# Sliding-window attention with the values as the stationary operand: two heads side by side on 64 array columns each, and the division by the denominators moved to ScalarE

## The chip, the cores and the metric

The program runs on one NeuronCore of a Trainium2 chip, in one launch. The metric is the device time in microseconds (us) of one execution. TensorE (PE in the profile, its weight loads PEld), VectorE (DVE), ScalarE (ACT), GpSimd (POOL) and SyncE (SP) each run their own instructions strictly in the order of the program and wait for one another through semaphores.

## The reference, cut to what matters

Four layers on 256 tokens of width 1024: two of a first kind, then two "hybrid" layers, each with a gated delta-rule branch, a sliding-window branch and a feed-forward part. The change is in the sliding-window branch, which has 16 query heads of width 64 on 2 key/value heads, blocks of 128 tokens, a window of 128 and one sink logit per head:

```python
def swa_sink_branch(q_in, k_in, v_in, positions, sinks):
    ...
    scores = jnp.einsum('bnqhgd,bnkhd->bnhgqk', qb, kw) * (SW_HEAD_DIM ** -0.5)
    ...
    scores = jnp.where(mask, scores, -jnp.inf)
    sink = sinks.astype(jnp.float32).reshape(SW_KV_HEADS, G)[None, None, :, :, None, None]
    m = jnp.maximum(jnp.max(scores, axis=-1, keepdims=True), sink)
    p = jnp.exp(scores - m)
    probs = p / (jnp.sum(p, axis=-1, keepdims=True) + jnp.exp(sink - m))
    o = jnp.einsum('bnhgqk,bnkhd->bnqhgd', probs.astype(vw.dtype), vw)
    return o.reshape(B, S, SW_Q_W)

def hybrid_layer_2(x, positions, ...):
    ...
    y_b = swa_sink_branch(sw_q, sw_k, sw_v, positions, sw_sinks) @ w_up_sw
```

## The kernel before

Every large product takes a 128x128 stationary tile and streams up to 512 columns. A weight matrix comes from memory in pieces of 256 rows by 512 columns (`raw`). ACT rounds a piece to `hi` (L284) and DVE takes the rest `lo` (L285), and the activations are kept as such a pair too (`lhi`, `llo`). A product is then three matmuls, L312 to L314 in `mm3`, or L353 to L355 in `proj_w`. Four split pieces are kept (`NSPLIT`).

Python writes the order of all engines ahead of time. `at(k, fn)` puts `fn` on a list for `k` steps from now, `tick(0.5)` after each three or six matmuls moves the clock on and emits what is due, and `feed` splits the next weight piece when a buffer is free. So attention, the delta rule and the projections stand interleaved in one fixed order per engine. `wk` hands out three PSUM buffers in turn, to scores (`sc`), transposes (`tp`, `pt`) and the delta rule's products (`pg`, `inv`) alike: PE writes the next one only when the reader of the third last is done.

A hybrid layer (`layer2`) calls `swa(g)` for the two groups of 8 heads; I number a layer's heads 0 to 15. For each head, `windowed` schedules four functions: `s_` (scores on PE at L495 and L496, mask and maximum on DVE at L500, `nm` at L1276), 1.5 steps later `e_` (two exponentials on ACT at L1284, which also leave the row sums in `den`; the sink's exponential `es` at L1287; their sum on POOL), at 2.8 `t_` (three transposes on PE at L507, copied by ACT at L509 to `ptS`), and at 3.7 `v_`. The columns of `e` are the keys of three pairs of blocks: query block 1 with key blocks 0 and 1, and query block 0 with key block 0. `v_` calls `pv_mm`: three matmuls with a 128x128 block of probabilities stationary and the 64 value columns streaming. After every fourth head DVE takes the reciprocal of the eight denominators (L1303) and multiplies `o` into `y` (L1305, twice); `y` lies in the buffer named `tok`. After the eighth head `to_lh` turns `y` with four PE transposes per token block (L371) and splits it (ACT L376, DVE L378) into `sw["lb"]`, the operand of the product with `w_up_sw`.

At the same places run the delta rule's steps: on DVE `eights` and `corner` (L1138 to L1155), `spread` (L1158), and the convolution's taps (six instructions of L993, which continue what ACT starts at L990); on PE `level_z` (L1167). The queries' own copies into `qk` alternate between ACT (L461) and DVE (L462).

Of the kernel before, what the change touches and what calls it, by code (L numbers as in the profile page):

```python
# [12 lines left out]
F32 = mybir.dt.float32  # L13
# [64 lines left out]
def body(ctx: ExitStack, tc: tile.TileContext, I, out, upto=None):  # L78
# [52 lines left out]
    def wk(shape, name="wk", tag="wk", bufs=3):  # L131
        return ps.tile(shape, F32, name=name, tag=tag, bufs=bufs)
# [98 lines left out]
    def at(k, fn):  # L231
        heapq.heappush(due, (clk[0] + k, seq[0], fn))
        seq[0] += 1
# [16 lines left out]
    def tiny(n, name="tiny", bufs=4):  # L250
        return sm.tile([128, n], F32, name=name, tag=f"{name}{n}", bufs=bufs)
# [202 lines left out]
    def into_stack(dst, r, tabs):  # L454


        def then(p, cols, t):
            for i in range(2):
                a, b = halves(i)
                h = dst[a, i:8:2, cols]  # L460
                S.activation(h, p[a], AF.Copy)  # L461
                V.tensor_tensor(out=dst[b, i:8:2, cols], in0=p[a], in1=h.bitcast(F32), op=ALU.subtract)  # L462
        return turned(r, tabs, then, 4)
# [40 lines left out]
    def probs_T(p):  # L504
        pt = wk([128, 384], "pt")
        for j in range(3):
            T.transpose(pt[:, j * 128:(j + 1) * 128], p[:, j * 128:(j + 1) * 128], ident)  # L507
        r = sm.tile([128, 384], F32, name="ptS", tag="ptS", bufs=2)
        S.activation(r, pt, AF.Copy)  # L509
        return r  # L510

    def pv_mm(o1, o0, pt, v, cols):
        T.matmul(o1, pt[:, 0:128], v[:, 0, cols], start=True, stop=False)
        T.matmul(o1, pt[:, 128:256], v[:, 1, cols], start=False, stop=True)
        T.matmul(o0, pt[:, 256:384], v[:, 0, cols], start=True, stop=True)

    def e_tile():
        return sm.tile([128, 384], F32, name="e", tag="e", bufs=3)

    def by_block(ap, n=4):  # L520
        return ap.rearrange("p (h t) -> p h t", t=2)
# [353 lines left out]
    def layer2(l, last):  # L875
# [388 lines left out]

        lane = [0.0]

        def windowed(q, g, y):
            st = {}

            def s_(h):  # L1270
                if h % 4 == 0:
                    st["den", h // 4] = tiny(8, "den")
                s, mx = scores(q[:, h, :], kTs[0][:, g, :], kTs[1][:, g, :], tb_("bs"))
                nm = tiny(2, "nm")
                hs = 8 * g + h
                V.tensor_scalar(nm, mx, -0.125, nsink[:, hs:hs + 1], op0=ALU.mult, op1=ALU.min)  # L1276
                st["s", h] = s, nm

            def e_(h):
                den, i, hs = st["den", h // 4], h % 4, 8 * g + h  # L1280
                s, nm = st.pop(("s", h))
                e = e_tile()
                for j, (a, b) in enumerate(SPL):
                    S.activation(e[:, a:b], s[:, a:b], AF.Exp, bias=nm[:, j:j + 1], scale=0.125,  # L1284
                                 accum_out=den[:, 2 * i + j:2 * i + j + 1])
                es = tiny(2, "es")
                S.activation(es, nm, AF.Exp, bias=sinks[:, 16 * l + hs:16 * l + hs + 1])  # L1287
                G.tensor_tensor(out=den[:, 2 * i:2 * i + 2], in0=den[:, 2 * i:2 * i + 2], in1=es, op=ALU.add)
                st["p", h] = e

            def t_(h):
                st["pt", h] = probs_T(st.pop(("p", h)))

            def v_(h):
                hh, i = h // 4, h % 4
                if i == 0:
                    st["o"] = wk([128, 4, 2, 64], "o", "o", 1)
                o = st["o"]
                pv_mm(o[:, i, 0, :], o[:, i, 1, :], st.pop(("pt", h)), vS, slice(64 * g, 64 * g + 64))
                if i < 3:  # L1300
                    return
                rd = tiny(8, "rd")
                V.reciprocal(rd, st["den", hh])  # L1303
                for j in range(2):
                    V.tensor_tensor(out=y[:, 1 - j, 256 * hh:256 * hh + 256].rearrange("p (h d) -> p h d", d=64),  # L1305
                                    in0=o[:, :, j, :],
                                    in1=rd.rearrange("p (h t) -> p t h", t=2)[:, j, :, None].to_broadcast([128, 4, 64]),
                                    op=ALU.mult)
                if hh == 1:
                    for t in range(2):  # L1310
                        at(1.6 + t, lambda t=t: to_lh(sw["lb"], y[:, t, :], 4 * g, t))

            for h in range(8):
                k = max(4, lane[0] - clk[0])
                at(k, lambda h=h: s_(h))
                at(k + 1.5, lambda h=h: e_(h))
                at(k + 2.8, lambda h=h: t_(h))
                at(k + 3.7, lambda h=h: v_(h))
                lane[0] = clk[0] + k + 2.1

        m1, fins, end = [], [], 0.0
# [7 lines left out]
        def swa(g):  # L1329
            q = qk_tile([8, 256], F32R)  # L1330
            if g == 0:
                sw["lb"] = new_lh()
            y, evac = into_stack(q, None, rope2)
            proj(lh, evac)
            windowed(q, g, y)

        for hh in range(2):
            qkn = dn_qk(hh)
# [206 lines left out]
```

## Time and profile before

| what | value |
|---|---|
| time of three runs, median | 1740.27 us (1738.24 to 1742.22) |
| the profiled execution: its time, its span | 1741.27 us, 1739.5 us |
| PE busy, PEld busy | 1705.6 us (98%), 1484.6 us (85%) |
| DVE, ACT, POOL busy | 1169.9 us (67%), 996.4 us (57%), 268.1 us (15%) |
| mean granted clock of TensorE | 0.994 |

The span runs from the first to the last instruction that the profiler recorded, and the execution's own time is 1.8 us longer. "Busy" counts instructions in flight. PE's matmuls overlap one another, so what a matmul costs is read from the distance between starts, and not from its duration. A matmul on plain fp32 operands shows as two records, each with a weight load of its own; a transpose shows as one.

### The profile page before, as it was taken

What the parts mean: (1) busy time and instruction counts of PE and PEld (TensorE: products, weight loads), DVE (VectorE), ACT (ScalarE), POOL (GpSimd) and SP (SyncE); (2) the same over time, 40 slices, a digit from 0 to 9 for tenths busy, and PEclk for the clock granted to TensorE, in tenths of its full rate; (3) what the DMA queues carried; (4) which work ended last, traced back from release to release, by engine and by line L of the source; (5) the groups of instructions that cost most, each with busy time, mean ns of one, the idle gap of its engine ahead of it and who ended that gap; (6) DMA issues with size and microseconds to landing.
All of it is one profiled execution on the core that took longest, in us unless ns stands there. A gap on an engine that the chain in (4) does not pass through costs nothing.

```text
span 1739.5 us, 26865 instructions
## 1 busy us (share of the span) xinstructions
PE 1705.6 (98%) x9865; PEld 1484.6 (85%) x9865; DVE 1169.9 (67%) x2189; ACT 996.4 (57%) x1786; POOL 268.1 (15%) x507
## 2 busy tenths in 40 slices
PE   8999999999999999999999999999999999999998
PEld 6788888888888888898889889998998888889997
DVE  5676776666777766788585676555788584775554
ACT  6666665466666654665665455445565666464443
POOL 2112321031123200320220000000320210010000
PEclk9999999999999999999999999999999999999999
DMA  6655465466655565554332655665554333646564
GB/s 206 196 173 167 152 189 173 159 195 181 177 164 155 172 192 174 168 166 134 96 104 86 197 167 182 194 193 170 160 170 140 87 102 93 198 158 195 184 184 140
DMA packets 158932, 282.27 MB, mean 162 GB/s; under 512 B 20560, under 2 KB 28496, under 8 KB 158800
## 3 DMA queue, kind: packets, MB, share of 16 engines
q1 hardware_dynamic: 157840, 277.83, 53.0%
q0 software_dynamic: 720, 2.62, 0.4%
q8 instruction: 78, 1.28, 0.3%
q14 instruction: 54, 0.44, 0.1%
q10 hardware_dynamic: 240, 0.09, 0.0%
HBM read 270.53 MB, written 1.59 MB: 156 GB/s over the span
## 4 chain that ended last, share of the span: by engine, by line
PE 51%; DVE 5%; issue 1%; ACT 1%; POOL 0%; DMA 0%; DVEq 0%; POOLq 0%; SPq 0%; ACTq 0%
PE acc L314 6%; PE acc L312 6%; PE acc L313 6%; PE acc L353 5%; PE acc L354 5%; PE acc L355 5%; PE facc L313 3%; PE facc L312 3%; PE facc L314 3%; DVE lo L285 2%; DVE hcv L993 1%; PE inv L1177 1%; PE inv L1167 1%; PE tp L371 1%; PE pt L507 1%
## 5 line engine op out<-in xcount | busy, mean ns | idle before, releaser
L285 DVE TENSOR_TENSOR lo<-raw,hi 128x1024 fp32r<-128x1024 f32 (+1 forms) x504 | 617.3, 1231 | 343.9 <-ACT hi L284 328.1
L284 ACT ACTIVATE hi<-raw 128x1024 fp32r<-128x1024 f32 (+1 forms) x504 | 527.3, 1052 | 357.5 <-PE acc L314 149.0
L312 PE MATMUL acc<-hi,lhi 128*128 128x512 f32 (+1 forms) x1344 | 550.4, 410 | 1.2 <-ACT lhi L385 1.2
L314 PE MATMUL acc<-hi,llo 128*128 128x512 f32 (+1 forms) x1344 | 526.2, 392 | 0.4 <-DVE llo L388 0.3
L313 PE MATMUL acc<-lo,lhi 128*128 128x512 f32 (+1 forms) x1344 | 524.2, 390 | 0.6 <-DVE lo L285 0.5
L314 PEld LDWEIGHTS acc<-hi,llo 128*128 128x128 f32 x1344 | 253.5, 189 | 57.4 <-DVE llo L388 3.4
L313 PEld LDWEIGHTS acc<-lo,lhi 128*128 128x128 f32 x1344 | 255.3, 190 | 41.3 <-DVE lo L285 2.0
L312 PEld LDWEIGHTS acc<-hi,lhi 128*128 128x128 f32 x1344 | 255.0, 190 | 39.7 <-ACT lhi L385 1.4
L353 PE MATMUL acc<-lhi,hi 128*128 128x256 f32 x832 | 239.1, 287 | 0.0
L355 PE MATMUL acc<-lhi,lo 128*128 128x256 f32 x832 | 235.4, 283 | 0.0
L354 PE MATMUL acc<-llo,hi 128*128 128x256 f32 x832 | 235.4, 283 | 0.0
L353 PEld LDWEIGHTS acc<-lhi,hi 128*128 128x128 f32 x832 | 159.5, 192 | 1.2 <-issue 0.4
L354 PEld LDWEIGHTS acc<-llo,hi 128*128 128x128 f32 x832 | 159.5, 192 | 0.7
L355 PEld LDWEIGHTS acc<-lhi,lo 128*128 128x128 f32 x832 | 159.4, 192 | 0.0
L312 PE MATMUL facc<-hi,fh 128*128 128x512 f32 x256 | 99.8, 390 | 0.0
L313 PE MATMUL facc<-lo,fh 128*128 128x512 f32 x256 | 99.8, 390 | 0.0
L314 PE MATMUL facc<-hi,fl 128*128 128x512 f32 x256 | 99.6, 389 | 0.0
L509 ACT ACTIVATE ptS<-pt 128x384 f32<-128x384 f32 x80 | 39.2, 490 | 82.0 <-PE pt L507 81.8
L546 POOL TENSOR_SCALAR pf<-pss 128x1 f32<-128x1 f32 x8 | 3.7, 458 | 467.6 <-ACT pj L860 467.6
L500 DVE CUSTOM_DVE_ANT_0 s<-sc,tab 128x256 f32<-128x256 f32 x192 | 60.4, 352 | 11.2 <-PE sc L496 10.6
L993 DVE SCALAR_TENSOR_TENSOR hcv<-acc,cw,hcv 128x255 f32<-128x255 f32 (+1 forms) x144 | 58.2, 475 | 1.5 <-ACT hcv L990 1.4
L314 PEld LDWEIGHTS facc<-hi,fl 128*128 128x128 f32 x256 | 48.1, 188 | 10.1
(306 smaller groups left out, 2206.9 us busy)
## 6 DMA issues: line engine op xcount, KB each, us to landing
raw<-in_w_in_dram SPq DMA_DIRECT2D x272, 512.0 KB, 3.8
raw<-in_w_ff_dram SPq DMA_DIRECT2D x128, 512.0 KB, 4.4
raw<-in_w_proj_a_dram SPq DMA_DIRECT2D x16, 512.0 KB, 3.9
raw<-in_w_proj_b_dram SPq DMA_DIRECT2D x16, 512.0 KB, 3.7
raw<-in_w_out_dram SPq DMA_DIRECT2D x16, 512.0 KB, 3.7
raw<-in_w_up_sw_dram SPq DMA_DIRECT2D x16, 512.0 KB, 3.7
raw<-in_w_up_dn_dram SPq DMA_DIRECT2D x16, 512.0 KB, 3.7
raw<-in_w_o_dram SPq DMA_DIRECT2D x16, 512.0 KB, 3.8
```

What stands on the lines that cost most here:

```text
L284: S.activation(hi[:, :, :o], raw[:, :, :o], AF.Copy)
L285: V.tensor_tensor(out=lo[:, :, :o], in0=raw[:, :, :o], in1=hi[:, :, :o].bitcast(F32), op=ALU.subtract)
L312: T.matmul(a, lh[0][:, c, sl], hi[:, cc, :n], start=first, stop=False)
L313: T.matmul(a, lh[0][:, c, sl], lo[:, cc, :n], start=False, stop=False)
L314: T.matmul(a, lh[1][:, c, sl], hi[:, cc, :n], start=False, stop=last)
L353: T.matmul(a, hi[:, c % 2, sl], lh[0][:, c, :], start=(c == 0 and m % 2 == 0), stop=False)
L354: T.matmul(a, hi[:, c % 2, sl], lh[1][:, c, :], start=False, stop=False)
L355: T.matmul(a, lo[:, c % 2, sl], lh[0][:, c, :], start=False, stop=(c == 7 and m % 2 == 1))
L371: T.transpose(p[:, a, :], src[:, a * 128:(a + 1) * 128], ident)
L500: V.tensor_tensor_reduce(s[:, a:b], sc[:, a:b], bias[:, a:b], 1.0, FMIN, ALU.add, ALU.max, accum_out=mx[:, j:j + 1])
L509: S.activation(r, pt, AF.Copy)
L993: V.scalar_tensor_tensor(ha[:, m, d:], a[:, m, :256 - d], tap(3 - d, m), ha[:, m, d:], op0=ALU.mult, op1=ALU.add)
```

## The change

`v_` now works on pairs of heads. The values (128 keys x 64) are stationary, the turned probabilities stream: for key block 0 the two query blocks that use it in one matmul of 256 columns, for key block 1 one matmul of 128 columns. The first head of a pair writes PSUM partitions 0 to 63, that is columns 0 to 63 of the array, the second one partitions 64 to 127. The result stands with the head's width on partitions already, in the layout of `sw["lb"]`, so `y`, `to_lh` and its transposes go. ACT and DVE split `o` straight into `sw["lb"]` (L1327, L1328).

Since queries are now on the free axis, the division comes earlier, on the probabilities, where queries are still on partitions: a new step `r_` (DVE: add `es` and `den`, L1292, then the reciprocal, L1293) and a new step `n_` (ACT: `e` times that reciprocal in place, in two pieces, L1299). `t_` moves from 2.8 to 4.6 steps, `v_` from 3.7 to 5.6. `e` has four buffers. POOL's addition goes. No DMA is added, removed or moved.

```diff
-        return sm.tile([128, 384], F32, name="e", tag="e", bufs=3)
+        return sm.tile([128, 384], F32, name="e", tag="e", bufs=4)
...
-                G.tensor_tensor(out=den[:, 2 * i:2 * i + 2], in0=den[:, 2 * i:2 * i + 2], in1=es, op=ALU.add)
+                st["p", h] = e, es
+
+            def r_(h):
+                rd, i, (e, es) = tiny(2, "mx"), h % 4, st["p", h]
+                V.tensor_tensor(out=rd, in0=st["den", h // 4][:, 2 * i:2 * i + 2], in1=es, op=ALU.add)
+                V.reciprocal(rd, rd)
+                st["p", h] = e, rd
+
+            def n_(h):
+                e, rd = st["p", h]
+                for j, (a, b) in enumerate(SPL):
+                    S.activation(e[:, a:b], e[:, a:b], AF.Copy, scale=rd[:, j:j + 1])
                 st["p", h] = e
...
-                pv_mm(o[:, i, 0, :], o[:, i, 1, :], st.pop(("pt", h)), vS, slice(64 * g, 64 * g + 64))
-                if i < 3:
+                if h % 2 == 0:
                     return
-                rd = tiny(8, "rd")
-                V.reciprocal(rd, st["den", hh])
...
+                for blk in range(2):
+                    for i, pt in enumerate(pts):
+                        w = o[64 * i:64 * i + 64, pr, :]
+                        if blk == 0:
+                            T.matmul(w.rearrange("p (t c) -> p t c", t=2), vS[:, 0, 64 * g:64 * g + 64], pt[:, 0:3:2, :],
+                                     start=True, stop=False)
+                        else:
+                            T.matmul(w[:, 0:128], vS[:, 1, 64 * g:64 * g + 64], pt[:, 1, :], start=False, stop=True)
...
-                        at(1.6 + t, lambda t=t: to_lh(sw["lb"], y[:, t, :], 4 * g, t))
+                    S.activation(hi, p, AF.Copy)
+                    V.tensor_tensor(out=lo, in0=p, in1=hi.bitcast(F32), op=ALU.subtract)
...
-                at(k + 2.8, lambda h=h: t_(h))
-                at(k + 3.7, lambda h=h: v_(h))
+                at(k + 2.6, lambda h=h: r_(h))
+                at(k + 3.0, lambda h=h: n_(h))
+                at(k + 4.6, lambda h=h: t_(h))
+                at(k + 5.6, lambda h=h: v_(h))
```

Three places show where the new steps come to stand. All are in the first hybrid layer where its first group of heads ends and the second begins. On DVE, from the `nm` of head 9 on, before:

```order
L1276 TENSOR_SCALAR nm<-mx,nsink 128x2
L993 SCALAR_TENSOR_TENSOR hcv<-acc,cw_80,hcv 128x255 x2
L993 SCALAR_TENSOR_TENSOR hcv<-acc,cw_80,hcv 128x254 x2
L993 SCALAR_TENSOR_TENSOR hcv<-acc,cw_80,hcv 128x253 x2
L285 TENSOR_TENSOR lo<-raw,hi 128x1024
L378 TENSOR_TENSOR llo<-tp,lhi 128x4x128
L1158 TENSOR_TENSOR Xi<-Y,tab 128x512
```

and now:

```order
L1276 TENSOR_SCALAR nm<-mx,nsink 128x2
L993 SCALAR_TENSOR_TENSOR hcv<-acc,cw_80,hcv 128x255 x2
L993 SCALAR_TENSOR_TENSOR hcv<-acc,cw_80,hcv 128x254 x2
L993 SCALAR_TENSOR_TENSOR hcv<-acc,cw_80,hcv 128x253 x2
L1292 TENSOR_TENSOR mx<-den,es 128x2
L1293 RECIPROCAL mx<-mx 128x2
L285 TENSOR_TENSOR lo<-raw,hi 128x1024
L1158 TENSOR_TENSOR Xi<-Y,tab 128x512
L1328 TENSOR_TENSOR llo<-o,lhi 128x2x128 x2
```

The denominators of head 8 stand behind the taps and right ahead of the weights' `lo`; heads 7 and 9 have the same neighbour behind them. On ACT, the same place, from the exponentials of head 8 on, before:

```order
L1284 ACTIVATE e,den<-s,nm 128x256
L1284 ACTIVATE e,den<-s,nm 128x128
L1287 ACTIVATE es<-nm,bv_sw_sinks_336 128x2
L990 ACTIVATE hcv<-acc,cw_80 128x256 x2
L509 ACTIVATE ptS<-pt 128x384
L284 ACTIVATE hi<-raw 128x1024
L376 ACTIVATE lhi<-tp 128x4x128
```

and now:

```order
L1284 ACTIVATE e,den<-s,nm 128x256
L1284 ACTIVATE e,den<-s,nm 128x128
L1287 ACTIVATE es<-nm,bv_sw_sinks_336 128x2
L509 ACTIVATE ptS<-pt 128x384
L990 ACTIVATE hcv<-acc,cw_80 128x256 x2
L1299 ACTIVATE e<-e,mx 128x256
L1299 ACTIVATE e<-e,mx 128x128
L284 ACTIVATE hi<-raw 128x1024
L1327 ACTIVATE lhi<-o 128x2x128 x2
```

The division of head 8 stands right ahead of the `hi` of the same weight piece. On PE, where the projection changes from `proj_w` to `proj`, before:

```order
L355 MATMUL acc<-lhi,lo 128x256
L507 MATMUL pt<-ident,e 128x128 x3
L312 MATMUL acc<-hi,lhi 128x512
L313 MATMUL acc<-lo,lhi 128x512
L314 MATMUL acc<-hi,llo 128x512
L371 MATMUL tp<-ident,tok 128x128 x4
L312 MATMUL acc<-hi,lhi 128x512
L313 MATMUL acc<-lo,lhi 128x512
L314 MATMUL acc<-hi,llo 128x512
L513 MATMUL o<-vS,ptS 128x64
L514 MATMUL o<-vS,ptS 128x64
L515 MATMUL o<-vS,ptS 128x64
```

and now:

```order
L355 MATMUL acc<-lhi,lo 128x256
L312 MATMUL acc<-hi,lhi 128x512
L313 MATMUL acc<-lo,lhi 128x512
L314 MATMUL acc<-hi,llo 128x512
L1317 MATMUL o<-ptS,vS 64x256 x2
L1320 MATMUL o<-ptS,vS 64x128 x2
L312 MATMUL acc<-hi,lhi 128x512
L313 MATMUL acc<-lo,lhi 128x512
L314 MATMUL acc<-hi,llo 128x512
```

Head 8's three transposes have moved 9 product matmuls down, past the next scores, the four transposes of `y` are gone, and two heads' value products are four instructions in a row.

## Rows read from the trace of the kernel before

**Rows 1.** The profile's page: busy time, and the granted clock in 40 slices.
```profile
PE 1705.6 (98%) x9865; PEld 1484.6 (85%) x9865; DVE 1169.9 (67%) x2189; ACT 996.4 (57%) x1786; POOL 268.1 (15%) x507
...
PEclk9999999999999999999999999999999999999999
```
**Rows 2.** Timeline of PE near 945: start us, duration us, instruction.
```profile
945.01 0.39 PE L314 MATMUL acc<-hi,llo 128*128 128x512 f32 x1
945.25 0.33 PE L513 MATMUL o<-vS,ptS 128*128 128x64 f32 x2
...
945.83 0.47 PE L312 MATMUL acc<-hi,lhi 128*128 128x512 f32 x1
946.14 0.39 PE L313 MATMUL acc<-lo,lhi 128*128 128x512 f32 x1
946.37 0.40 PE L314 MATMUL acc<-hi,llo 128*128 128x512 f32 x1
```
**Rows 3.** Timeline of PE near 949: four transposes of `y`.
```profile
948.65 0.40 PE L314 MATMUL acc<-hi,llo 128*128 128x512 f32 x1
948.89 0.60 PE L371 MATMUL tp<-ident,tok 128*128 128x128 f32 x4
...
949.56 0.39 PE L313 MATMUL acc<-lo,lhi 128*128 128x512 f32 x1
```
**Rows 4.** Timeline of PE near 780: fp32 matmuls of 256 and 128 columns.
```profile
780.09 0.60 PE L1085 MATMUL pg<-qk 128*128 128x256 f32 x2
780.52 0.38 PE L1086 MATMUL pg<-qk 128*128 128x128 f32 x2
...
780.86 0.28 PE L354 MATMUL acc<-llo,hi 128*128 128x256 f32 x1
780.98 0.28 PE L355 MATMUL acc<-lhi,lo 128*128 128x256 f32 x1
```
**Rows 5.** Timeline near 1263: the same two shapes on 8 array columns.
```profile
1262.89 0.60 PE L942 MATMUL tp<-tab,gd 128*8 128x256 f32 x2
...
1263.33 0.38 PE L943 MATMUL tp<-tab,gd 128*8 128x128 f32 x2
...
1263.86 0.28 PE L354 MATMUL acc<-llo,hi 128*128 128x256 f32 x1
```
**Rows 6.** Busy us of the engines in two stretches of 10 us, from 890.
```profile
890.00:900.00 10.00, 9.89 (x75) 8.85 (x74) 9.04 (x22) 7.59 (x19) 1.31 (x2) 1.00 0.31 71
900.00:910.00 10.00, 9.14 (x63) 8.04 (x62) 9.96 (x25) 6.33 (x19) 1.29 (x2) 1.00 0.33 101
```
**Rows 7.** Timeline of PE at two waits; in brackets idle time and releaser.
```profile
886.83 0.63 PE L446 MATMUL tp<-ident,tok 128*128 128x128 f32 x4 [0.33 <-DVE mx L500]
...
903.65 0.52 PE L507 MATMUL pt<-ident,e 128*128 128x128 f32 x3 [0.86 <-DVE llo L378]
```
**Rows 8.** Timeline of DVE from 895 to 910.
```profile
895.62 0.42 DVE L500 CUSTOM_DVE_ANT_0 s<-sc,tab 128x256 f32<-128x256 f32 x1
...
897.57 0.20 DVE L1303 RECIPROCAL rd<-den 128x8 f32<-128x8 f32 x1
897.87 0.76 DVE L1305 TENSOR_TENSOR tok<-o,rd 128x256 f32<-128x256 f32 x2
...
902.82 0.69 DVE L378 TENSOR_TENSOR llo<-tp,lhi 128x512 fp32r<-128x512 f32 x1
...
909.50 0.42 DVE L500 CUSTOM_DVE_ANT_0 s<-sc,tab 128x256 f32<-128x256 f32 x1
```
**Rows 9.** Timeline of ACT: a scaling by columns, and three rows of 893 to 898.
```profile
769.21 0.80 ACT L1081 ACTIVATE D<-D,cj 128x256 f32<-128x256 f32 x2 [2.85 <-POOL cj L1036]
...
893.38 1.05 ACT L284 ACTIVATE hi<-raw 128x1024 fp32r<-128x1024 f32 x1
...
896.56 0.51 ACT L1284 ACTIVATE e<-s,nm 128x256 f32<-128x256 f32 x1 [2.13 <-DVE nm L1276]
...
897.64 0.82 ACT L990 ACTIVATE hcv<-acc,cw 128x256 f32<-128x256 f32 x2
```

More of the change, by code (lines that the diff above doesn't have):

```diff
@@ L1265, in layer2, with windowed @@
         lane = [0.0]
-        def windowed(q, g, y):
+        def windowed(q, g):
             st = {}
@@ L1289, in e_ @@
+            def n_(h):
+                e, rd = st["p", h]
+                for j, (a, b) in enumerate(SPL):
+                    S.activation(e[:, a:b], e[:, a:b], AF.Copy, scale=rd[:, j:j + 1])
                 st["p", h] = e
             def t_(h):
-                st["pt", h] = probs_T(st.pop(("p", h)))
+                st["pt", h] = probs_T(st.pop(("p", h))).rearrange("p (a c) -> p a c", a=3)
             def v_(h):
-                hh, i = h // 4, h % 4
-                if i == 0:
-                    st["o"] = wk([128, 4, 2, 64], "o", "o", 1)
@@ L1298, in v_ @@
-                o = st["o"]
-                pv_mm(o[:, i, 0, :], o[:, i, 1, :], st.pop(("pt", h)), vS, slice(64 * g, 64 * g + 64))
-                if i < 3:
-                    return
-                rd = tiny(8, "rd")
-                V.reciprocal(rd, st["den", hh])
[L1304 to L1308, printed above, removed]
@@ L1309, in v_ @@
-                if hh == 1:
-                    for t in range(2):
-                        at(1.6 + t, lambda t=t: to_lh(sw["lb"], y[:, t, :], 4 * g, t))
+                if h % 2 == 0:
+                    return
+                if h % 4 == 1:
+                    st["o"] = wk([128, 2, 256], "o", "o", 1)
+                o, pr = st["o"], h // 2 % 2
+                pts = [st.pop(("pt", h - 1)), st.pop(("pt", h))]
+                for blk in range(2):
[6 more added lines that the diff above has]
+                            T.matmul(w[:, 0:128], vS[:, 1, 64 * g:64 * g + 64], pt[:, 1, :], start=False, stop=True)
@@ L1313, in windowed @@
+                if pr == 0:
+                    return
+                c = 4 * g + 2 * (h // 4)
+                for t in range(2):
+                    hi, lo = [x[:, c:c + 2, 128 * t:128 * t + 128] for x in sw["lb"]]
+                    p = o[:, :, 128 - 128 * t:256 - 128 * t]
+                    S.activation(hi, p, AF.Copy)
+                    V.tensor_tensor(out=lo, in0=p, in1=hi.bitcast(F32), op=ALU.subtract)
             for h in range(8):
@@ L1332, in swa @@
                 sw["lb"] = new_lh()
-            y, evac = into_stack(q, None, rope2)
-            proj(lh, evac)
-            windowed(q, g, y)
+            proj(lh, into_stack(q, None, rope2)[1])
+            windowed(q, g)
         for hh in range(2):
```

## The prediction

> **What bounds the kernel now.** I read the page first: PE is busy 98% of the span, every other engine at most 67%, and the granted clock stands at its top digit in all 40 slices [rows 1]. So there is no clock to win back, and time can come only from PE's own work or from what PE waits for. All of PE's idle time is 1739.5 − 1705.6 = 33.9 us [rows 1]. That average hides one stretch in each hybrid layer. The windows of 10 us from 890 on, where the delta rule's steps, the weight pieces and heads 7 to 11 meet, show DVE busy 9.04 and then 9.96 us of 10, while PE falls to 9.14 [rows 6]. PE's timeline there shows it waiting for DVE, 0.33 us for a head's maximum and 0.86 us for an `llo` [rows 7]. Both waits come through the three buffers of `wk`. So the kernel has two limits: PE nearly everywhere, and DVE for some 30 us in each of the two hybrid layers. A step put into that stretch is paid on DVE; a step saved outside it is paid on PE.
>
> **PE's work.** Two layers of 16 heads are 32 heads and 16 pairs. A head's three value matmuls first: from the last L314 ahead of them (945.01) to the next L314 behind (946.37) are 1.36 us [rows 2]; an `mm3` product's steps L312, L313, L314 take 0.23 us each from start to start (946.14 to 946.37), so 0.69 of it is the product's own, and 0.67 us is the values'. 32 heads make 21.4 us. The four transposes of `y`: 0.91 us from L314 to L313 around them, less two plain steps of 0.23, is 0.45 us [rows 3]; 8 groups give 3.6 us. Removed: 25.0 us.
>
> Added are, for each pair, two fp32 matmuls of 256 columns and two of 128. One of each on the whole array costs 0.77 us from the first start to the next product, less the 0.12 us of that product's own step: 0.65 us [rows 4]. The same two shapes on a tile of 8 array columns take 0.97 us, 0.20 more [rows 5], which I read as the price of going into a narrower tile and back. No row shows two tiles at work together, so I bound a pair from both sides: one after the other 2 × 0.65 + 0.20 = 1.50 us; wholly beside each other 0.65 + 0.20 = 0.85 us. The four instructions are issued in turn, first half, second half, each as two records, and a 256-column record of one half can start beside the other's; but nothing here shows that it does. I take the middle, about 1.25: 16 pairs, 20.0 us. PE's work changes by −5.0 us (bounds −1.0 and −11.4). The turned probabilities, their three transposes per head and the scores stay as they are.
>
> The Trainium skill, page "TensorEngine Tiling (Array Packing)", section "Key Properties", says that different tiles load weights and multiply in parallel. By it a pair would cost 0.85 us and PE's work would fall by 11.4; no row of before has two such tiles side by side, so it stands as a rival below.
>
> **Work on the other engines.** POOL loses 32 additions that nobody on the path waits for. ACT gains a division of each head: two instructions that scale by a column took 0.80 us [rows 9], 32 × 0.80 = 25.6 us, and the `hi` of `o` at half of a two-instruction group of 0.82 us [rows 9], against the `hi` of `y`, which goes. ACT is at 57% [rows 1], so the amount is no matter; where it stands is. DVE gains per head the addition and the reciprocal. Small instructions that depend on one another start 0.2 to 0.3 us apart [rows 8]; I take 0.45 us for both. It gains the subtraction of `o`, 0.38 (half of a 0.76 group) to 0.42 us for 128x256 from PSUM [rows 8], and loses the reciprocal and two multiplications of every four heads (897.57 to 898.54, 0.97 us) and the `llo` of `y` (0.69 us) [rows 8]. No DMA moves, and weight pieces are split well ahead of their product, so PE's operands of the projections don't get late by a fraction of a microsecond.
>
> **Where the new steps stand.** This is the term that decides. In the crowded stretch `r_` of heads 7, 8 and 9 stands on DVE right ahead of a weight piece's `lo`, and `n_` of the same head stands on ACT right ahead of that same piece's `hi`. `lo` needs `hi`, `hi` stands behind `n_`, and `n_` needs `r_`. So DVE ends the reciprocal, and then waits for 0.80 us of division [rows 9] and 1.05 us of rounding [rows 9] before it can go on: 1.85 us idle, each time, on an engine that had 1.00 us idle in 20 [rows 6]. Before, nothing tied that `hi` to DVE, and it could run while DVE was still at the taps. Three such places: 5.55 us. Near head 4 that head's division stands on ACT ahead of the `hi` of the first four heads' `o` (L1327), for which DVE's L1328 waits: 0.80 of division and most of the two `hi` (0.82 a pair [rows 9]), 1.5 us; near head 5 I allow 0.35, less than half a division. Together 7.4 us. Queued behind each of these on DVE are the mask and maximum of the next head, the taps and `spread`; behind the maximum stand `nm`, the exponentials (ACT already waited 2.13 us for `nm` [rows 9]) and, through `wk`, PE.
>
> DVE's plain work up to the scores of head 11, before at 909.50 [rows 8], grows by 6 × 0.45 (`r_` of heads 4 to 9) + 4 × 0.42 − 2 × 0.97 − 2 × 0.69 = +1.1 us. So DVE gets there 8.5 us later, less the 1.00 us that it stood idle in the 20 us from 890 [rows 6]: 7.5 us. Other ways to absorb it I don't see: PE has only the three buffers of `wk` as lead, and already stood waiting on them at 903.65 [rows 7].
>
> What PE saves inside the stretch doesn't count, since PE is waiting there: six heads' values and two groups of transposes, 6 × 0.67 + 2 × 0.45 = 4.9 us, against three pairs, 3.75; 1.15 us of a layer's 2.5. Outside 1.35 us per layer is saved.
>
> **The sum.** The second hybrid layer runs the same code; I take it as the same. 2 × 7.5 − 2 × 1.35 = +12.3 us. On the profiled execution, 1741.27, that is 1753.6. That execution lies 1.0 us above the median of the runs shown, 1740.27, and on the median it is 1752.6: I forecast **1753 us**, slower.
>
> **Rivals.**
>
> *The stall doesn't come* (the other side). For it: DVE is at 67% over all [rows 1]; the two waits of [rows 7] hang on a maximum and on an `llo` that goes away, so they may shrink; and PE may run far enough behind its lists that 1.85 us of DVE disappear. Against it: 9.96 of 10 [rows 6]. Then only PE's work counts, −5.0: 1735 us, with the bounds of a pair 1729 to 1739. It decides where the added stall is under 1.35 us per layer, that is if not even one of the three 1.85 us places gets through to PE. Chance 0.25.
>
> *The halves run side by side, and the stall comes.* A pair costs 0.85 us; per layer PE saves 5.7, of which 4.9 − 3 × 0.85 = 2.35 inside the stretch; outside 3.35. 2 × 7.5 − 2 × 3.35 = +8.3: 1749 us. This is the Trainium skill's rule, cited above. For it: the two halves write different PSUM partitions and read different `ptS`. Against: in [rows 5] a tile of 8 columns was no cheaper than the whole array, though nothing ran beside it. Chance 0.20.
>
> *The stalls add up fully and the halves run one after the other.* `t_` of heads 7 and 8 stands on PE at about the place where DVE finishes `r_`, so PE's in-order queue waits for the division too, and with PE the next scores, which hold DVE's next maximum: a loop through three engines, at which each of the four or five places costs another half microsecond, some 10 us per layer. With a pair at 1.50 nothing is saved outside worth counting (0.1 us). 2 × 10: +20, 1760 us. Chance 0.15.
>
> *Gain and stall cancel*: stalls of 1 to 3 us per layer, within 3.5 us of the time before. Chance 0.08.
>
> **How the numbers follow.** The forecast itself has 0.32, with the two rivals that keep the stall 0.67 for slower. Its own range runs from three bare 1.85 us places with side by side halves, 2 × 5.55 − 6.7 = +4.4 (1745), to the full loop with some more at it (1763). The range must also take in part of the faster case: from 1733, which leaves out the third or so of the faster case in which the halves run well side by side, to 1763. A measurement of this kernel tells some 0.2%, 3.5 us, from no change. Faster 0.25, same 0.08, slower 0.67.
>
> **What would show it.** In the profile after: the distance from the first start of a value group to the product behind it, 0.85, 1.25 or 1.50 us above a plain step; on DVE, ahead of the `lo` behind each of the three reciprocals, an idle time near 1.85 us released by ACT's `hi`; the maximum of head 11 at 917 instead of 909.50; PE idle at new waits for DVE or for ACT's division, together 12 to 18 us more than 33.9; no transposes of `y`; the granted clock unchanged. I am wrong if DVE's idle time in the stretch stays near 1 us, if `hi` had been waiting for something else already, or if the idle time is there and PE never waits for it, because what stands ahead on PE is longer than I think. A clock below the top digit would be a cause that I have not counted.

## The result, and the profile after

The changed kernel takes 1766.36 us (median of 4, 1762.8 to 1768.06) against 1741.22 us before (median of 4), a ratio of 1.0145 (95% interval 1.0124 to 1.0165): slower, as forecast, but by 25 us instead of 12, and above the range. The profiled execution has a span of 1763.8 us.

The page, first busy time, then the granted clock in 40 slices; they answer to [rows 1]:

```profile
PE 1710.7 (97%) x9769; PEld 1477.2 (84%) x9769; DVE 1171.9 (66%) x2237; ACT 1020.3 (58%) x1858; POOL 260.1 (15%) x475
...
PEclk9999999999999999998989999999999989999999
```

PE stood idle for 53.1 us instead of 33.9, and three slices have lost the top digit of the clock. PE's busy time did not fall although it has less to do, since at a lower clock the same work takes longer: a product step of 0.12 us at the full clock takes 0.21 near 892, where the clock is 0.50. The windows around the crowded stretch (span, then busy us of PE, PEld, DVE, ACT and POOL, granted clock, DMA share, GB/s) show both:

```profile
885.00:895.00 10.00, 6.05 (x39) 5.13 (x38) 7.75 (x25) 6.38 (x16) 0.00 (x0) 0.83 0.32 101
895.00:905.00 10.00, 9.35 (x67) 7.75 (x66) 7.79 (x21) 6.03 (x18) 0.00 (x0) 1.00 0.38 81
905.00:915.00 10.00, 6.70 (x37) 5.47 (x36) 6.28 (x16) 4.56 (x13) 0.00 (x0) 0.96 0.28 92
915.00:925.00 10.00, 6.34 (x24) 4.68 (x22) 5.62 (x19) 6.58 (x16) 0.00 (x0) 0.53 0.18 52
```

Nobody is full here any more, neither DVE (9 to 10 of 10 us in [rows 6]) nor ACT: they wait for one another in turn. PE's waits (start, duration, instruction, in brackets idle time and who ended it), where [rows 7] had 0.33 and 0.86 us:

```profile
889.87 0.67 PE L446 MATMUL tp<-ident,tok 128*128 128x128 f32 x4 [3.95 <-DVE mx L500]
900.59 0.62 PE L507 MATMUL pt<-ident,e 128*128 128x128 f32 x3 [0.57 <-ACT e L1299]
907.33 0.62 PE L507 MATMUL pt<-ident,e 128*128 128x128 f32 x3 [1.14 <-ACT e L1299]
913.34 1.31 PE L1167 MATMUL inv<-Xi,LA 128*128 128x128 f32 x8 [2.16 <-ACT ptS L509]
917.71 0.90 PE L507 MATMUL pt<-ident,e 128*128 128x128 f32 x3 [1.77 <-ACT e L1299]
920.49 2.08 PE L1167 MATMUL inv<-Xi,LA 128*128 128x128 f32 x8 [1.88 <-ACT Z L1169]
```

The longest of them, 3.95 us for the maximum of head 7, stands ahead of the first triangle of reciprocal, division, `hi` and `lo` (the reciprocal of head 7 comes at 899.77).

DVE in the same stretch. First the waits near heads 4 and 5, 1.69, 0.45, 0.52 and 0.42 us, together 3.08 where the prediction had 1.5 and 0.35. The 1.85 us that the prediction looked for stand there three times, as 1.88 (the releaser named at the first had long been done; it is ACT's `hi`, as at the others), and at the end the maximum of head 11, which [rows 8] had at 909.50:

```profile
880.50 0.42 DVE L1328 TENSOR_TENSOR llo<-o,lhi 128x256 fp32r<-128x256 f32 x1 [1.69 <-ACT lhi L1327]
881.38 0.42 DVE L1328 TENSOR_TENSOR llo<-o,lhi 128x256 fp32r<-128x256 f32 x1 [0.45 <-ACT lhi L1327]
882.33 1.23 DVE L285 TENSOR_TENSOR lo<-raw,hi 128x1024 fp32r<-128x1024 f32 x1 [0.52 <-ACT hi L284]
...
886.52 1.23 DVE L285 TENSOR_TENSOR lo<-raw,hi 128x1024 fp32r<-128x1024 f32 x1 [0.42 <-ACT hi L284]
...
901.81 1.23 DVE L285 TENSOR_TENSOR lo<-raw,hi 128x1024 fp32r<-128x1024 f32 x1 [1.88 <-PE acc L354]
...
908.55 1.23 DVE L285 TENSOR_TENSOR lo<-raw,hi 128x1024 fp32r<-128x1024 f32 x1 [1.88 <-ACT hi L284]
...
918.93 1.23 DVE L285 TENSOR_TENSOR lo<-raw,hi 128x1024 fp32r<-128x1024 f32 x1 [1.88 <-ACT hi L284]
...
920.07 0.42 DVE L500 CUSTOM_DVE_ANT_0 s<-sc,tab 128x256 f32<-128x256 f32 x1
```

And ACT, with two waits that nobody had counted: its second `hi` of `o` waits for DVE's first `lo`, 0.49 and then 1.96 us.

```profile
880.96 0.39 ACT L1327 ACTIVATE lhi<-o 128x256 fp32r<-128x256 f32 x1 [0.49 <-DVE llo L1328]
...
910.75 0.38 ACT L1327 ACTIVATE lhi<-o 128x256 fp32r<-128x256 f32 x1 [1.96 <-DVE llo L1328]
```

The value products themselves, with the products around them:

```profile
877.38 0.40 PE L314 MATMUL acc<-hi,llo 128*128 128x512 f32 x1
877.71 0.65 PE L1317 MATMUL o<-ptS,vS 128*64 128x256 f32 x4
878.19 0.39 PE L1320 MATMUL o<-ptS,vS 128*64 128x128 f32 x4
878.51 0.39 PE L353 MATMUL acc<-lhi,hi 128*128 128x256 f32 x1
878.73 0.28 PE L354 MATMUL acc<-llo,hi 128*128 128x256 f32 x1
```

From L314 to L354 are 1.35 us, less 0.23 and 0.12 for the two products' own steps: a pair costs 1.00 us. The four records of 256 columns (L1317) take 0.48 us from their first start to that of L1320, about what two take on the whole array (0.43 us in [rows 4]): the halves do work side by side. The Trainium skill (page "TensorEngine Tiling (Array Packing)", "Key Properties") says that different tiles work in parallel, and this trace agrees. The pair lies 0.15 above the 0.85 that the prediction worked out for it; 0.10 of that lies ahead of its first start (877.71, where 877.38 + 0.23 would be a plain step), which the measure of [rows 5], taken from the first start, leaves out. The other pairs that stand between products at the full clock cost 0.99 or 1.00 us by the same working, but for that of heads 6 and 7 in either layer: 1.70 us. In the first layer its second half starts at 903.3, when ACT has copied that head's `ptS` (902.74 for 0.47 us).

### The profile page after: what moved, and what is told of

The parts are those of the page before. It is cut to its first block, busy times and chain, and to the rows that moved or that the text cites. A ratio compares the mean times of both kernels' runs of the same rounds, so it can differ in the third digit from the quotient of the medians.

```text
span 1763.8 us, 26763 instructions
## 1 busy us (share of the span) xinstructions
PE 1710.7 (97%) x9769; PEld 1477.2 (84%) x9769; DVE 1171.9 (66%) x2237; ACT 1020.3 (58%) x1858; POOL 260.1 (15%) x475
## 4 chain that ended last, share of the span: by engine, by line
PE 45%; DVE 8%; ACT 4%; issue 1%; DMA 1%; POOL 1%; DVEq 0%; SPq 0%; POOLq 0%; ACTq 0%
PE acc L312 5%; PE acc L314 5%; PE acc L313 5%; PE acc L353 4%; PE acc L355 4%; PE acc L354 4%; PE facc L312 3%; PE facc L313 3%; PE facc L314 3%; DVE lo L285 3%; DVE hcv L993 2%; PE inv L1167 1%; PE inv L1177 1%; ACT hi L284 1%; PE tp L371 1%
## 5 line engine op out<-in xcount | busy, mean ns | idle before, releaser
L312 PE MATMUL acc<-hi,lhi 128*128 128x512 f32 (+1 forms) x1344 | 551.2, 410 | 1.7 <-ACT lhi L385 1.7
L314 PE MATMUL acc<-hi,llo 128*128 128x512 f32 (+1 forms) x1344 | 527.8, 393 | 0.7 <-DVE llo L388 0.6
L314 PEld LDWEIGHTS acc<-hi,llo 128*128 128x128 f32 x1344 | 254.9, 190 | 58.4 <-DVE llo L388 3.8
L312 PEld LDWEIGHTS acc<-hi,lhi 128*128 128x128 f32 x1344 | 256.0, 190 | 43.0 <-ACT lhi L385 2.2
L353 PE MATMUL acc<-lhi,hi 128*128 128x256 f32 x832 | 240.2, 289 | 0.0
L355 PE MATMUL acc<-lhi,lo 128*128 128x256 f32 x832 | 236.5, 284 | 0.0
L354 PE MATMUL acc<-llo,hi 128*128 128x256 f32 x832 | 236.5, 284 | 0.0
L353 PEld LDWEIGHTS acc<-lhi,hi 128*128 128x128 f32 x832 | 160.5, 193 | 1.8 <-issue 1.2
L354 PEld LDWEIGHTS acc<-llo,hi 128*128 128x128 f32 x832 | 160.6, 193 | 0.6
L355 PEld LDWEIGHTS acc<-lhi,lo 128*128 128x128 f32 x832 | 160.5, 193 | 0.0
L312 PE MATMUL facc<-hi,fh 128*128 128x512 f32 x256 | 99.8, 390 | 0.0
L314 PE MATMUL facc<-hi,fl 128*128 128x512 f32 x256 | 99.6, 389 | 0.0
L314 PEld LDWEIGHTS facc<-hi,fl 128*128 128x128 f32 x256 | 48.1, 188 | 10.1
```

The source lines that it names most:

```text
L312: T.matmul(a, lh[0][:, c, sl], hi[:, cc, :n], start=first, stop=False)
L314: T.matmul(a, lh[1][:, c, sl], hi[:, cc, :n], start=False, stop=last)
L353: T.matmul(a, hi[:, c % 2, sl], lh[0][:, c, :], start=(c == 0 and m % 2 == 0), stop=False)
L354: T.matmul(a, hi[:, c % 2, sl], lh[1][:, c, :], start=False, stop=False)
L355: T.matmul(a, lo[:, c % 2, sl], lh[0][:, c, :], start=False, stop=(c == 7 and m % 2 == 1))
```

## Where the time stands, measured on the products

Product matmuls come in the same order in every version. I number them (7296 of L312 to L314 and L353 to L355) and compare each one's start, counted from the start of the span, with that in the kernel before. The 3301st stands ahead of the first hybrid layer's stretch (885.21 us before), the 3601st behind it (987.48), the 5701st and the 6001st likewise in the second layer. Lags in us, each from the run's one profiled execution, and the growth across each stretch:

```
run                        3301st 3601st 5701st 6001st   growth in layer 1, 2
changed kernel              -0.66 +12.79 +10.44 +24.36   13.45 13.92
e1_no_division              -4.26  -1.75  -2.68  -0.17    2.51  2.51
e2_division_pool            +0.83  +8.42  +8.77 +16.42    7.59  7.65
e3_hi_first                 -0.80  +9.67  +7.95 +18.40   10.48 10.45
e4_old_values               -0.80  +9.78  +8.75 +19.14   10.58 10.38
e5_division_after_hi        -2.85  +0.22  -1.49  +1.62    3.07  3.11
e6_division_dve             -1.98  +0.57  -1.79  +0.78    2.55  2.57
e7_no_division_hi_first     +1.17  +1.06  -1.47  -1.53   -0.10 -0.06
e9_after_hi_later_t         -2.40  +1.74  -0.07  +4.11    4.13  4.18
e10_dve_later_t             -2.35  -0.15  -2.02  +1.82    2.20  3.84
e11_dve_add_on_pool         -3.51  -0.46  -2.58  -1.15    3.05  1.43
e12_fill_zero               -0.87  +8.10  +6.68 +15.68    8.96  9.00
e13_pool_later_t            +1.69  +3.42  +2.41  +4.74    1.73  2.33
e14_old_values_after_hi     -0.33  +4.95  +3.92  +9.23    5.28  5.30
```

The lag of the 3301st differs between runs by up to 6 us, but that of the 3000th, ahead of all heads, differs as much (−2.9 to +4.0), and up to there the kernels do the same; so I read the growth, which leaves this out. For the changed kernel 13.45 + 13.92 − 0.66 − 2.35 (between the stretches) = +24.36: the whole loss arises in the two stretches, alike in both.

## Experiments

**The division left out**, with its three edits to the schedule:

```diff
-                st["p", h] = e, es
+                st["p", h] = e
-                at(k + 2.6, lambda h=h: r_(h))
-                at(k + 3.0, lambda h=h: n_(h))
```

> The changed kernel without the division: no addition, no reciprocal on DVE, no scaling on ACT; transposes and value products stay at their late places. It leaves the division by the denominators out altogether. Theory A (the division ties DVE's `lo` to ACT's `hi`, and PE's waits and its lowered clock follow from that): PE's saving is left, two layers of about 4.5 us, so 1730 to 1737 us. Theory B (the late transposes, the paired value matmuls or the subtraction of `o` by turns of ACT and DVE hold PE up): 1750 us or more.

1743.16 us, ratio 1.0008 (0.9998 to 1.0017). Between both theories: the division explains most of the loss, but without it PE's saving still doesn't show. 2.51 us per stretch are left.

**The division on POOL.**

```diff
-                    S.activation(e[:, a:b], e[:, a:b], AF.Copy, scale=rd[:, j:j + 1])
+                    G.tensor_scalar(e[:, a:b], e[:, a:b], rd[:, j:j + 1], None, op0=ALU.mult)
```

> The changed kernel, with the same two scalings of each head on POOL instead of ACT; DVE's order is unchanged, ACT loses the two scalings. Theory A (what costs is that ACT's `hi` stands behind the division): DVE's idle 1.88 us ahead of `lo` goes to about nothing, 1735 to 1748 us. Theory C (what costs is the latency that a division adds to each head, so that PE's transposes wait for it): POOL needs longer than ACT's 0.80 us for it, so PE waits at least as long, 1765 us or more.

1757.64 us, ratio 1.0098 (1.0083 to 1.0113), between the two expectations: freeing ACT's queue gives 6 us per stretch back (13.45 to 7.59, 13.92 to 7.65), but PE then waits for POOL, 1.91, 2.10, 0.80 and 2.16 us in the first layer.

**Both `hi` first**: ACT writes both copies of `o` before DVE's two subtractions. No engine's own order changes.

```diff
                 for t in range(2):
-                    hi, lo = [x[:, c:c + 2, 128 * t:128 * t + 128] for x in sw["lb"]]
-                    p = o[:, :, 128 - 128 * t:256 - 128 * t]
-                    S.activation(hi, p, AF.Copy)
-                    V.tensor_tensor(out=lo, in0=p, in1=hi.bitcast(F32), op=ALU.subtract)
+                    S.activation(sw["lb"][0][:, c:c + 2, 128 * t:128 * t + 128], o[:, :, 128 - 128 * t:256 - 128 * t], AF.Copy)
+                for t in range(2):
+                    hi, lo = [x[:, c:c + 2, 128 * t:128 * t + 128] for x in sw["lb"]]
+                    V.tensor_tensor(out=lo, in0=o[:, :, 128 - 128 * t:256 - 128 * t], in1=hi.bitcast(F32), op=ALU.subtract)
```

> The changed kernel with both `hi` copies of `o` written ahead of both subtractions; each engine's order is unchanged, only ACT's second `hi` no longer waits for DVE's first `lo`. That wait was 0.49 and 1.96 us in the first layer's stretch. Theory B (this turn-taking is a main cause): 5 us or more are given back, 1755 to 1761 us. Theory A: it is a small part, 1762 to 1766 us.

1759.27 us, ratio 1.0104 (1.0089 to 1.0119). Theory B holds: 7 us by the emission order of four instructions, 3.0 and 3.5 us per stretch. DVE's first `lo` reads the first `hi` slice, ACT's second `hi` writes the other slice of the same buffer, in which the two lie interleaved; I read the wait as one for the whole region, which the data did not need. That it is gone with the other order is shown, what in the program's dependences made it is not. ACT's two waits are gone in its trace, DVE's three of 1.88 us are not (1.88, 1.88 and 1.87).

**The old values with the new division**: `v_`, `y` and `to_lh` as before, the multiplication by the reciprocal replaced by a copy, `r_`, `n_` and the late steps as in the change.

```diff
-                rd = tiny(8, "rd")
-                V.reciprocal(rd, st["den", hh])
-                    V.tensor_tensor(out=y[...], in0=o[:, :, j, :], in1=rd..., op=ALU.mult)
+                    V.tensor_copy(y[:, 1 - j, 256 * hh:256 * hh + 256].rearrange("p (h d) -> p h d", d=64), o[:, :, j, :])
```

> The kernel before with the division alone moved: addition, reciprocal and ACT's scaling of the probabilities, transposes and value products at the late places, but three value matmuls per head with the probabilities stationary, DVE copying `o` to `y`, and the four transposes of `y`. Theory A: all the stalls of the changed kernel and none of its saving on PE (about 4.5 us per layer), 1768 to 1780 us. Theory B (the value products in pairs, or the way `o` is split, hold PE up): 1740 to 1750 us.

1760.33 us, ratio 1.0115 (1.01 to 1.0131), below what Theory A said. It lacks the 7 us of turn-taking (it has no L1327), and its greater work on PE falls in part into time in which PE would wait: from 830 to 970 us PE is idle 7.8 us, against 10.8 in the run above. Its growth per stretch, 10.58 and 10.38, is close to that of the run above: the division makes it with either form of the values. That the late steps alone don't make it is shown further down, by the run with them and without division.

**The division behind `hi`** on ACT, all work the same (with both `hi` first, as in all that follow but the last):

```diff
-                at(k + 3.0, lambda h=h: n_(h))
+                at(k + 3.6, lambda h=h: n_(h))
```

> The changed kernel with both `hi` copies of `o` first (as in the run before, 1759.3 us) and ACT's division moved from 3.0 to 3.6 steps, so that on ACT it stands behind the weight piece's `hi` and right ahead of the next head's exponentials. All work is the same. Theory A (what costs is the triangle reciprocal, division, `hi`, `lo`): DVE's idle times of 1.88 us go, and most of the 10.5 us per layer with them: 1738 to 1750 us. Theory C (the division's latency in each head's own chain costs, wherever it stands): PE gets the probabilities no earlier, 1755 us or more.

1744.08 us, ratio 1.0009 (0.9997 to 1.002): 0.6 steps of one function are worth 15 us against the run with both `hi` first. Behind its reciprocals DVE no longer waits; the `lo` starts 0.11 us after the reciprocal's start, where it was 2.04 (899.77 to 901.81):

```profile
900.83 0.17 DVE L1293 RECIPROCAL mx<-mx 128x2 f32<-128x2 f32 x1
900.94 1.23 DVE L285 TENSOR_TENSOR lo<-raw,hi 128x1024 fp32r<-128x1024 f32 x1
```

PE still waits at its transposes for ACT's division, as if Theory C held a part:

```profile
895.87 0.62 PE L507 MATMUL pt<-ident,e 128*128 128x128 f32 x3 [1.33 <-ACT e L1299]
901.65 0.62 PE L507 MATMUL pt<-ident,e 128*128 128x128 f32 x3 [0.89 <-ACT e L1299]
908.48 0.62 PE L507 MATMUL pt<-ident,e 128*128 128x128 f32 x3 [1.40 <-ACT e L1299]
```

**The division on DVE**, the first diff of POOL with `V.tensor_scalar`.

> The changed kernel with both `hi` copies of `o` first and the two scalings of each head on DVE, behind its own reciprocal, instead of on ACT. Theory A: no engine waits for another between reciprocal and division, and ACT's `hi` is free; DVE pays some 0.6 us of work per head in the full stretch instead of 1.88 us of waiting, so about half of the 10.5 us per layer comes back: 1744 to 1753 us. Theory C: the chain of a head is hardly shorter: 1756 us or more.

1742.86 us, ratio 1.0002 (0.9989 to 1.0016), a little better than expected: work on the fuller engine costs less than a wait through the emptier one. Against ACT's division behind `hi` (1.0009) it makes no clear difference.

**No division and both `hi` first**, the first and the third edit together.

> The changed kernel without any division (left out altogether: no addition, reciprocal or scaling) and with both `hi` copies of `o` first. If division and turn-taking of `hi` and `lo` are two separate costs that add up: 1743.2 less about 6.5, 1734 to 1739 us, below the kernel before. If the turn-taking costs only where the division has made ACT late: 1741 to 1744 us, no change against the run without division.

1736.1 us, ratio 0.9969 (0.9957 to 0.9981). The two costs add up, and the growth across the stretches is nothing (−0.10, −0.06), so the late steps and the paired values cost nothing there. With these steps I take this, some 5.4 us below the kernel before, as the most that a better place of the division could give.

**PE's idle time filled**, first try: small matmuls into unread columns of the scores' buffer.

```diff
+            for _ in range(n):
+                T.matmul(sc[:, 384:512], q[:, 0:128], kh[:, 128:256], start=True, stop=True)
```

> The changed kernel with both `hi` copies of `o` first, and idle PE filled: in each hybrid layer 26 small matmuls (128 columns, into columns of the scores' PSUM buffer that nobody reads) ahead of the four `tok` transposes that waited 3.41 us, and 5, 10 and 24 ahead of the transposes of heads 7, 8 and 9 that waited 0.59, 1.11 and 2.59 us. They add work that no result needs. Theory K (the granted clock falls after PE has stood idle, and the low clock itself costs up to 3.2 us per layer): the clock stays full from 885 to 925 us and the time falls to 1752 to 1757 us. If the low clock costs nothing because PE would wait anyway: 1758 to 1763 us.

1784.0 us, ratio 1.0242 (1.0225 to 1.0259). It tells nothing of the clock: the filling waited for DVE's read of that buffer itself and started when the idle time was over (3.31 us), 4.54 us of extra work on the path.

```profile
888.39 4.54 PE L137 MATMUL sc<-kTh,qk 128*128 128x128 f32 x26 [3.31 <-DVE mx L513]
```

**Filled with zeros**: fp32 matmuls of a block of zeros, added to the product that is running, which wait for nothing.

```diff
+            T.matmul(busy["acc"], tb_("bb")[:, 0:128], tb_("mi"), start=False, stop=False)
```

> The changed kernel with both `hi` copies of `o` first (1759.3 us) and PE's idle time filled with fp32 matmuls that add zero to the running product and wait for nothing: 6, 1, 2, 5 and 4 of 256 columns ahead of five waits of 3.41, 0.59, 1.11, 2.59 and 2.16 us, by 0.43 us each 7.7 us of the 9.9 us of idle time per layer. They add work that no result needs. Theory K (the granted clock falls because PE stood idle, and the low clock itself costs time): the clock stays full there and up to 3.2 us per layer comes back, 1752 to 1757 us. If the low clock costs nothing, because PE would wait for the same engines anyway: 1758 to 1762 us with a full clock.

1756.81 us, ratio 1.0074 (1.0056 to 1.0092), against 1.0104 (1.0089 to 1.0119) unfilled. The two intervals just touch, but the growth falls in both layers, from 10.5 to 9.0 us per stretch. The windows of the unfilled kernel, and then of the filled one:

```profile
885.00:895.00 10.00, 6.59 (x44) 5.45 (x43) 7.85 (x22) 6.37 (x15) 0.00 (x0) 0.83 0.23 76
...
915.00:925.00 10.00, 7.84 (x44) 6.34 (x45) 4.42 (x12) 8.34 (x22) 0.00 (x0) 0.83 0.28 89
```

```profile
885.00:895.00 10.00, 9.19 (x68) 8.17 (x67) 7.85 (x22) 6.38 (x15) 0.00 (x0) 1.00 0.26 82
...
915.00:925.00 10.00, 9.57 (x66) 7.90 (x67) 5.95 (x16) 8.28 (x22) 0.00 (x0) 1.00 0.38 107
```

With PE kept at work the clock stays at 2.4 GHz, and work that nobody needs makes the kernel faster. About 1.5 us per stretch is what the low clock itself costs in this kernel; the rest of the stall is waiting. The clock is low twice in the unfilled kernel, from 890 to 894 and from 917 to 921. What the filled one wins in the first of these is lost at the next wait, which ends at the same time in both (first the unfilled kernel, then the filled one, in which L507 is L519):

```profile
899.83 0.62 PE L507 MATMUL pt<-ident,e 128*128 128x128 f32 x3 [0.59 <-ACT e L1299]
899.77 0.62 PE L519 MATMUL pt<-ident,e 128*128 128x128 f32 x3 [1.61 <-ACT e L1315]
```

Only the second, behind the last wait, is paid.

**Later transposes**, to take away PE's waits for the division: 5.4 and 6.4 steps instead of 4.6 and 5.6, with ACT's division behind `hi`, with DVE's, and with DVE's and the addition back on POOL.

```diff
-                at(k + 4.6, lambda h=h: t_(h))
-                at(k + 5.6, lambda h=h: v_(h))
+                at(k + 5.4, lambda h=h: t_(h))
+                at(k + 6.4, lambda h=h: v_(h))
```

> The run with ACT's division behind `hi` (1744.1 us), with the transposes moved from 4.6 to 5.4 steps and the value products from 5.6 to 6.4. There PE still waited at the transposes for ACT's division, 0.45, 1.33, 0.89 and 1.40 us in each layer. If those waits are on the path: about 8 us less, 1734 to 1739 us, near the run without division and below the kernel before. If they only stand in for waits on DVE that come next: 1741 to 1745 us.

> The run with the division on DVE (1742.9 us), with the same later transposes and value products. PE waited there for DVE's division, 2.10 and 0.57 us in the first layer, 0.94, 0.35 and 1.56 in the second. If those waits are on the path: 1735 to 1740 us; if DVE's load in the stretch is what holds PE: 1741 to 1744 us.

> As the run above, with the addition of the sink's exponential back on POOL, so that DVE loses one small instruction (about 0.2 us) per head. If DVE's load in the stretch is the limit: 1 to 3 us below the run above; if not, the same within a microsecond.

1747.15, 1744.08 and 1742.45 us; ratios 1.0022 (1.0011 to 1.0032), 1.0006 (0.9995 to 1.0016) and 0.9993 (0.9982 to 1.0003). The waits at the transposes only stood in for others: in the first of the three PE waits for DVE instead.

```profile
886.42 0.52 PE L507 MATMUL pt<-ident,e 128*128 128x128 f32 x3 [1.50 <-DVE mx L500]
889.75 0.38 PE L495 MATMUL sc<-kTh,qk 128*128 128x256 f32 x1 [1.39 <-DVE qk L462]
```

The third also has this edit, and the division on DVE:

```diff
+                G.tensor_tensor(out=den[:, 2 * i:2 * i + 2], in0=den[:, 2 * i:2 * i + 2], in1=es, op=ALU.add)
-                V.tensor_tensor(out=rd, in0=st["den", h // 4][:, 2 * i:2 * i + 2], in1=es, op=ALU.add)
-                V.reciprocal(rd, rd)
+                V.reciprocal(rd, es)
```

The addition off DVE gave 1.6 us in the medians, a difference in the expected direction, though the two intervals overlap.

**Addition and division on POOL**, only the reciprocal on DVE, transposes at 5.6 and values at 6.6; the edit is against the last of the three above.

```diff
-                    V.tensor_scalar(e[:, a:b], e[:, a:b], rd[:, j:j + 1], None, op0=ALU.mult)
+                    G.tensor_scalar(e[:, a:b], e[:, a:b], rd[:, j:j + 1], None, op0=ALU.mult)
-                at(k + 5.4, lambda h=h: t_(h))
-                at(k + 6.4, lambda h=h: v_(h))
+                at(k + 5.6, lambda h=h: t_(h))
+                at(k + 6.6, lambda h=h: v_(h))
```

> The changed kernel with both `hi` copies of `o` first, the addition and the scaling of the probabilities on POOL, only the reciprocal left on DVE, transposes at 5.6 and value products at 6.6 steps, so that PE has some 1 step more until it needs what POOL divided (it waited 0.8 to 2.2 us for it when the transposes stood at 4.6). If what is left of the division's cost (1742 to 1744 us against 1736.1 without division) is load on DVE and ACT: 1736 to 1740 us. If it is the longer chain itself, or POOL slowed by DVE's work: 1742 to 1750 us.

1741.23 us, ratio 0.9998 (0.9988 to 1.0009): between the two expectations, and no better than the kernel before.

**The old values with the division behind `hi`**, the edit of 3.0 to 3.6 made to the fourth run.

> The kernel before with the division alone moved (1760.3 us: three value matmuls per head, `y` and its transposes kept), with ACT's division at 3.6 steps, behind the weight piece's `hi`. Only the new values part is missing against the run of 1744.1 us. If the place of ACT's division costs the same 15 us with the old values, and PE's saving by the new ones is some 5 us: 1744 to 1751 us. If the place matters only together with the paired values and the split of `o`: 1756 us or more.

1751.29 us, ratio 1.006 (1.0042 to 1.0078). The place of the division costs with the old values too, but 9 us and not the same 15. Against e5 (1.0009) the paired values are worth 0.5%, about 9 us, which is PE's saving worked out with the measured pair, 25.0 − 16 × 1.00 = 9.0 us. But the two intervals allow anything from some 4 to 14 us, and PE stands idle longer in e5's trace (7.1 us from 830 to 970, against 5.6 here), so that a saving of 9.0 us should show as about 6. The run without division says it better: it is 5.4 us below the kernel before (3.3 to 7.5), although PE is idle 4.1 us from 830 to 970, against 2.0 before, and as much longer in the second layer, some 4.1 us more in the two; 5.4 + 4.1 = 9.5 us.

## Why the prediction was right in kind and wrong in size

*PE's work.* The pair was put at 1.25 us, in the middle of its bounds, and measures 1.00: PE saves 9.0 us, not 5.0, and the run without division bears that out with some 9.5. This error made the forecast too high, not too low. Between the stretches 2.35 us were gained where 1.35 was forecast; not all of that is PE's saving, since e4 and e14, with the old values at the late steps, gain 1.03 there as well.

*The triangle of reciprocal, division, `hi` and `lo`.* Right in mechanism and in its unit: 1.85 us forecast, 1.88 measured, at all three places, and moving the division by 0.6 steps took them away. That edit gave back 7.4 us in the first layer (10.48 to 3.07), but it moved the division of every head, that of head 4 too, which stood ahead of L1327. The 3350th product, 895.63 us before and 899.26 now, stands ahead of the first triangle and splits the growth:

```
growth in the first layer     3301st to 3350th   3350th to 3601st
changed kernel                       4.28               9.17
e3_hi_first                          3.66               6.82
e5_division_after_hi                 1.00               2.07
e7_no_division_hi_first              0.00              -0.10
```

So 2.7 of the 7.4 us came back near heads 4 to 6 and 4.7 at the triangles, with what the low clock costs behind them; 5.55 was forecast for the three.

*The step that failed* is the list of what else holds DVE and ACT up. Its term for heads 4 and 5, 1.5 and 0.35 us, was too small: DVE was idle 3.08 us there, PE's longest wait follows (3.95 us; 1.48 in e5, where DVE waits less there, 0.50 and 0.19 us), and 4.28 us were lost ahead of the first triangle. Two costs were not in the sum at all: 3.0 and 3.5 us per layer for the turn-taking of `hi` and `lo`, which I had as a chain of two copies and one subtraction, and not as ACT waiting for DVE in its turn (0.49 and 1.96 us); and 3.2 us per layer that the division costs even behind `hi` (e5 against e7). The sum was 7.5 us per layer; measured 13.45 and 13.92, in the first layer 3.0 for turns, 7.4 for the division's place, 3.2 for the rest of the division and −0.1 for what is left without it.

*The absorption*, −1.0 us, was not measured by itself. The maximum of head 11 came 10.6 us later than before, at 920.07, not 7.5 us later, at 917.

*The clock* was forecast unchanged, and a lower one named as a cause not counted. It did change: before, no slice was under the top digit [rows 1]; after, windows of 1 us show 0.50, that is 1.2 GHz, from 891 to 893 and from 915 to 924, each behind waits of PE of 2 to 4 us. In the version with both `hi` first it costs some 1.5 us per stretch of 10.5. No run fills the changed kernel itself, where the clock is low for longer, so its share there stays open.

*The rivals.* The one with full stalls (1760 us) came nearest, but by another sum: it had the halves one after the other. PE's waits for the division that it named did come (0.57, 1.14 and 1.77 us), but later transposes, which took such waits away, made the kernel no faster (e9, e10). The one with the halves side by side (1749 us) had the right pair. The faster one needed less than 1.35 us of stall per layer; e7 shows that it is what would have come with no division in the way.

*Open:* why a part of the division's cost remains at each of its better places, 3.1 us per stretch on ACT behind `hi`, 2.6 on DVE, 1.7 and 2.3 on POOL with later transposes. Taking it off ACT (e6), off ACT and, but for the reciprocal, off DVE (e13), or giving it more time (e9 to e11) each moves the wait to another place. A version with the whole work that is clearly faster than the kernel before was not found; the best stands at 0.9993 (0.9982 to 1.0003).

## What to carry to other kernels

When a step on one engine feeds a step on another, look at what stands right behind each of them in its queue: if those two depend on each other as well, every pass costs the sum of both, here 1.88 us, and moving one of them past its neighbour changes no work. Emit all copies that one engine makes before the other engine's uses of them, when slices of one buffer are written by one and read by the other. Price work that is moved to an idle engine by whom it makes wait, and not by that engine's share: 0.8 us on ACT, at 57%, cost more ahead of `hi` than the same work on DVE in its fullest stretch.

## What the hardware showed that I had not expected

PE's clock came down after waits of 2 to 4 us and stayed at 1.2 GHz for some microseconds into the work behind them; filling the waits with matmuls that change nothing kept it up and gained about 5 us net (1.0104 to 1.0074). Not every such wait did it: in e11 the granted clock fell behind a wait of 2.24 us, in e10 it stayed at 1.00 behind one of 2.27. In the version that was filled, the low clock ahead of another wait cost nothing, as its two rows show. And POOL's division was slower beside some of DVE's work: the same two instructions took 1.50 us while DVE stood idle and 2.86 us beside DVE's `lo` and `spread`.

```profile
907.12 2.86 POOL L1299 TENSOR_SCALAR e<-e,mx 128x256 f32<-128x256 f32 x2 [4.62 <-ACT lhi L1327]
...
947.53 1.50 POOL L1299 TENSOR_SCALAR e<-e,mx 128x256 f32<-128x256 f32 x2 [6.72 <-PE inv L1167]
```

Beside the mask and maximum of another head (875.99) they took 1.51 us, so not all of DVE's work slows them.
